# Gate and up by Strassen's seven products on token halves, and T5 biases loaded from DRAM by each mixer

## Chip, cores and metric

One core of a Trainium2 chip. The metric is the device time of one execution in microseconds, the median of the runs. Matmuls run on TensorE (PE in the profile, its weight loads PEld), elementwise work on VectorE (DVE), ScalarE (ACT) and GpSimd (POOL); SyncE (SP) issues most DMAs.

## The reference, cut to what matters

Two blocks run behind each other on 512 tokens of 1024 channels. The first has two layers, each a feed-forward, a mixer of three attentions, and a second feed-forward; the second block (adaptive norms, two more mixers, squared-ReLU networks) is not touched by the change, except for the pools that its first tiles come from.

```python
def _swiglu(x, w_gate, w_up, w_down):
    return (jax.nn.silu(x @ w_gate) * (x @ w_up)) @ w_down      # w_gate, w_up: 1024 x 2816

for l in range(DEPTH):                                          # DEPTH = 2
    x = x + 0.5 * _swiglu(_rmsnorm(x, ffn1_norm[l]), ffn1_w_gate[l], ffn1_w_up[l], ffn1_w_down[l])
    h = _rmsnorm(x, mix_norm[l])
    ...                                                         # three attentions, two with a T5 bias table
    x = x + jnp.concatenate([out_a, out_b, out_c], axis=-1) @ w_out[l]
    x = x + 0.5 * _swiglu(_rmsnorm(x, ffn2_norm[l]), ffn2_w_gate[l], ffn2_w_up[l], ffn2_w_down[l])
```

## The kernel before, in words

The activations lie transposed, eight chunks of 128 channels by 512 tokens. Every float32 product is made of three matmuls of a reduced float32 type (`mm3`, L136): weight and activation are each split in a rounded part (hi) and the rest (lo), and hi x hi, hi x lo and lo x hi are summed in PSUM. `weights` (L144) loads a weight block of 128 x 1024 into a ring of three raw tiles, casts hi on ACT (L149) and subtracts lo on DVE (L142), each in rings of two.

`ffn` (L357) runs 22 steps `up(f)` over the blocks of 128 hidden units. A step loads a gate and an up block, makes 8 chunks x 3 matmuls of 512 columns for each, and `gated` multiplies both by the norm's row factor R, applies Silu to the gate, multiplies, and splits the product into hi and lo (five DVE operations of 512 and two of ACT, counting the split). After 9, 17 and 22 steps `down` multiplies the finished hidden blocks into the eight output chunks; `residual` (L340) adds each to x and, in the last `down`, `push` (L319) makes hi and lo of the next norm's input (L323 on ACT, L325 on DVE) and adds its squares (ACT, then POOL for chunks 1 to 5, DVE for the others). There are four feed-forwards, so 88 steps `up` and 96 output chunks of `down`.

Beside this, `pump` takes a step of background work after each step f > 0 and before each chunk of the first two `down`s: first and foremost `adaln`, 96 units of a DMA of 512 KB and two DVE passes over 1024 elements (L832), which the second block needs; and, from step 2 of the very first feed-forward on, `bias_tables`, which spreads the T5 table over diagonals (DVE copies at L258), writes it skewed to DRAM and reads it back into two persistent tiles `bias_a` and `bias_b` (24 KB a partition), both DMAs on ACT's queue (L267 is the read). `mixer1` uses these tiles. The order in which instructions stand on each engine is made by a planner from program order and readiness, not by hand; each engine then works strictly in that order, and a tile's slot is taken again when its last reader is done.

Of the kernel before, what the change touches and what calls it, by code (L numbers as in the profile page):

```python
# [17 lines left out]
T = 512  # L18
# [106 lines left out]
class Net:  # L125
    def __init__(self, tc, ins, out):
        self.tc, self.nc, self.ins, self.out = tc, tc.nc, ins, out
        self.bg = []
        self.pre = None


    def mm(self, ps, lhsT, rhs, start, stop):
        self.nc.tensor.matmul(ps, lhsT, rhs, start=start, stop=stop)  # L133

    def mm3(self, ps, w, x, start, stop):
        (wh, wl), (xh, xl) = w, x  # L136
        self.mm(ps, wh, xh, start, False)
        self.mm(ps, wh, xl, False, False)
        self.mm(ps, wl, xh, False, stop)
# [4 lines left out]
    def weights(self, src, kc, m=128):  # L144
# [7 lines left out]
        return [(hi[:, k * m:(k + 1) * m], lo[:, k * m:(k + 1) * m]) for k in range(kc)]  # L152

# [85 lines left out]
    def bias_tables(self):  # L239

        nc, tc = self.nc, self.tc
        LA, LB = 384, 640
        with tc.tile_pool(name="boot", bufs=1, reuse_waits="tile") as bp:
# [4 lines left out]
            for L, top, h0, dmax, dst, n in ((LA, 255, 0, 128, self.bias_a, 256), (LB, 511, 8, 512, self.bias_b, 512)):  # L248
                v = bp.tile([128, 8, L], F32, name="v")
# [4 lines left out]
                while d < dmax:  # L254
                    e = d
                    while e < dmax and bk[e] == bk[d]:
                        e += 1
                    nc.vector.tensor_copy(v[:, :, top - e + 1:top - d + 1],  # L258
                                          tab[:, h0:h0 + 8, bk[d]:bk[d] + 1].to_broadcast([128, 8, e - d]))
                    d = e  # L260
                    if d < 16 and d % 4 == 0:
                        yield
                yield
                for h in range(8):
                    s = self.dp.tile([1, 128 * (L + 1)], F32, name="scr%d_%d" % (L, h))
                    nc.scalar.dma_start(s.rearrange("o (p l) -> (o p) l", l=L + 1)[:, :L], v[:, h, :])
                    nc.scalar.dma_start(dst[:, h, :],  # L267
                                        s[:, 127:127 + 128 * L].rearrange("o (p l) -> (o p) l", l=L)[:, :n])
                    if h % 4 == 3:
                        yield  # L270
# [47 lines left out]
    def push(self, d, g):  # L318

        nc = self.nc  # L320
        x = self.x[:, d, :]
        hi = self.xsp.tile([128, T], F32R, name="xs")
        nc.scalar.activation(hi, x, AF.Copy, scale=self.vecs[:, g + d:g + d + 1])  # L323
        lo = self.xsp.tile([128, T], F32R, name="xs")
        nc.vector.scalar_tensor_tensor(lo, x, self.vecs[:, g + d:g + d + 1], hi.bitcast(F32),  # L325
                                       op0=OP.mult, op1=OP.subtract)
        self.xn.append((hi, lo))
# [5 lines left out]
        else:  # L333
            (nc.gpsimd if d < 6 else nc.vector).tensor_tensor(self.acc[:, :T], self.acc[:, :T], sq, op=OP.add)

# [3 lines left out]
    def residual(self, d, ps, scale, g):  # L339
        self.nc.vector.scalar_tensor_tensor(self.x[:, d, :], ps, scale, self.x[:, d, :], op0=OP.mult, op1=OP.add)  # L340
        if g == "final":
            self.square_acc(self.lat, d)
            if d == 0:
                self.acc2 = self.xsp2.tile([128, T], F32, name="xslat", bufs=16)
# [12 lines left out]
    def ffn(self, l, which, nxt, hook=None):  # L357
        nc = self.nc
        gu, dn = self.ins["gu%d" % which], self.ins["dn%d" % which]
        with ExitStack() as es:  # L360
            ap = es.enter_context(self.tc.tile_pool(name="act", bufs=20, reuse_waits="tile"))
# [5 lines left out]
            h, late = {}, []  # L367
            R = y = None

            def up(f):  # L370
                nonlocal R, y
                ws = self.pre or [self.weights(gu[l, f, i], 8) for i in range(2)]
                self.pre = None
                ps = [self.psum(), self.psum()]
                if f == 0:
                    for k in range(8):
                        for w, p in zip(ws, ps):
                            self.mm3(p, w[k], xs[k], k == 0, k == 7)
                    y = self.rstd_y(self.acc, 4, D)
                    late.append((0, ps))  # L380
                    return
                for w, p in zip(ws, ps):
                    for k in range(8):
                        self.mm3(p, w[k], xs[k], k == 0, k == 7)
                if f == 1:
                    R = self.rstd_rows(y, 4)
                    gated(*late.pop())
                gated(f, ps)

            def gated(f, ps):  # L390
# [1706 lines left out]
```

## Time and profile before

| | us |
|---|---|
| median of 3 runs | 3663.9 (3657.01 to 3667.29) |
| the profiled execution | 3660.74 |
| its span from first to last instruction | 3658.7 |
| PE busy | 3576.8 |
| DVE busy | 2235.9 |
| ACT busy | 1492.9 |
| POOL busy | 165.9 |

In time the first block's feed-forwards run from 0 to 380, 612 to 976 and 976 to 1338, and 1571 to 1930 us; its mixers lie between, at 380 to 612 and 1338 to 1571; the rest is the second block. Busy time of PE is modelled, since matmuls overlap: the distance between starts says what one costs in a stream. DVE's and ACT's instructions that follow without a wait begin before the one ahead has ended, so there too starts are compared. A window's line gives the busy time and the number of instructions of each engine in that stretch, and the granted clock of TensorE, 1.00 for 2.4 GHz and 0.50 for 1.2 GHz.

### The profile page before, as it was taken

What the parts mean: (1) busy time and instruction counts of PE and PEld (TensorE: products, weight loads), DVE (VectorE), ACT (ScalarE), POOL (GpSimd) and SP (SyncE); (2) the same over time, 40 slices, a digit from 0 to 9 for tenths busy, and PEclk for the clock granted to TensorE, in tenths of its full rate; (3) what the DMA queues carried; (4) which work ended last, traced back from release to release, by engine and by line L of the source; (5) the groups of instructions that cost most, each with busy time, mean ns of one, the idle gap of its engine ahead of it and who ended that gap; (6) DMA issues with size and microseconds to landing.
All of it is one profiled execution on the core that took longest, in us unless ns stands there. A gap on an engine that the chain in (4) does not pass through costs nothing.

```text
span 3658.7 us, 47782 instructions
## 1 busy us (share of the span) xinstructions
PE 3576.8 (98%) x18706; PEld 3036.4 (83%) x18706; DVE 2235.9 (61%) x4146; ACT 1492.9 (41%) x2562; POOL 165.9 (5%) x186
## 2 busy tenths in 40 slices
PE   8999999999999999999999999999999989999999
PEld 6888887888888888878888888888888878798887
DVE  6576696767676649765446776643333578875443
ACT  4223574322322247542234656532122357763222
POOL 1000002000000010110000000100000101010000
PEclk9999999999999999999999999999999999999999
DMA  6354322445344432133332002111111310022222
GB/s 228 118 165 144 98 70 87 160 147 175 128 157 155 160 116 78 57 115 95 97 96 87 35 30 73 58 61 61 64 64 64 109 44 19 24 70 98 98 98 92
DMA packets 115473, 356.52 MB, mean 97 GB/s; under 512 B 12464, under 2 KB 23088, under 8 KB 114736
## 3 DMA queue, kind: packets, MB, share of 16 engines
q1 hardware_dynamic: 106432, 341.32, 28.2%
q10 hardware_dynamic: 8816, 12.15, 1.1%
q8 instruction: 147, 2.41, 0.3%
q14 instruction: 78, 0.64, 0.1%
HBM read 340.84 MB, written 12.58 MB: 97 GB/s over the span
## 4 chain that ended last, share of the span: by engine, by line
PE 89%; DVE 6%; ACT 3%; issue 1%; DMA 1%; ACTq 0%; SPq 0%; DVEq 0%
PE mm L133 77%; PE o L133 4%; PE s L133 4%; PE pt L1136 1%; DVE wlo L142 1%; PE mm L1749 1%; PE pt L662 1%; PE pt L133 1%; DVE xs L325 0%; ACT whi L149 0%; DVE u L883 0%; DVE xslat L885 0%; PE mm L1032 0%; DVE m L610 0%; ACT s L1743 0%
## 5 line engine op out<-in xcount | busy, mean ns | idle before, releaser
L133 PE MATMUL mm<-xs,whi 128*128 128x512 f32 (+1 forms) x3840 | 1189.7, 391 | 11.8 <-ACT whi L149 8.5
L149 ACT CAST whi<-wraw 128x1024 fp32r<-128x1024 f32 (+3 forms) x528 | 542.1, 1027 | 1583.2 <-PE mm L133 1261.5
L133 PEld LDWEIGHTS mm<-xs,whi 128*128 128x128 f32 x3840 | 717.6, 189 | 160.1 <-ACT whi L149 10.3
L133 PE MATMUL mm<-h,whi 128*128 128x512 f32 (+1 forms) x2944 | 820.8, 371 | 2.0 <-ACT whi L149 2.0
L142 DVE TENSOR_TENSOR wlo<-wraw,whi 128x1024 fp32r<-128x1024 f32 (+3 forms) x528 | 631.5, 1196 | 299.7 <-ACT whi L149 295.2
L133 PE MATMUL mm<-xs,wlo 128*128 128x512 f32 (+1 forms) x1920 | 748.3, 390 | 7.8 <-DVE wlo L142 7.7
L133 PEld LDWEIGHTS mm<-h,whi 128*128 128x128 f32 x2944 | 535.0, 188 | 108.7 <-ACT whi L149 2.2
L133 PE MATMUL mm<-h,wlo 128*128 128x512 f32 (+1 forms) x1472 | 515.4, 371 | 2.1 <-DVE wlo L142 2.1
L133 PEld LDWEIGHTS mm<-xs,wlo 128*128 128x128 f32 x1920 | 362.5, 189 | 87.0 <-DVE wlo L142 12.7
L133 PE MATMUL mm<-xslat,whi 128*128 128x512 f32 x1024 | 333.7, 403 | 6.6 <-DVE xslat L885 2.6
L133 PEld LDWEIGHTS mm<-h,wlo 128*128 128x128 f32 x1472 | 263.8, 188 | 42.6 <-DVE wlo L142 2.7
L832 DVE CUSTOM_DVE_ANT_0 junk<-wraw,silu_c 128x1024 f32<-128x1024 f32 x192 | 234.7, 1222 | 95.2 <-DMA wraw<-in_ada_w 93.8
L911 DVE SCALAR_TENSOR_TENSOR x<-mm,mod,x 128x512 f32<-128x512 f32 (+1 forms) x96 | 67.7, 706 | 282.3 <-PE mm L133 282.3
L133 PE MATMUL mm<-xslat,wlo 128*128 128x512 f32 x512 | 203.4, 398 | 0.7 <-DVE wlo L142 0.7
L133 PEld LDWEIGHTS mm<-xsctx,whi 128*128 128x128 f32 x944 | 171.6, 189 | 37.7 <-ACT w L1100 2.6
L133 PEld LDWEIGHTS mm<-xslat,whi 128*128 128x128 f32 x1024 | 167.2, 189 | 37.4 <-DVE xslat L885 5.4
L133 PE MATMUL mm<-xsctx,whi 128*128 128x256 f32 x944 | 191.6, 286 | 0.7 <-ACT w L1100 0.6
L340 DVE SCALAR_TENSOR_TENSOR x<-mm,x 128x512 f32<-128x512 f32 x144 | 99.2, 689 | 132.0 <-PE mm L133 131.9
L394 DVE TENSOR_TENSOR t<-mm,R 128x512 f32<-128x512 f32 x88 | 60.8, 691 | 138.4 <-PE mm L133 138.3
L392 DVE TENSOR_TENSOR t<-mm,R 128x512 f32<-128x512 f32 x88 | 60.7, 690 | 134.4 <-PE mm L133 134.4
L133 PE MATMUL mm<-xsctx,wlo 128*128 128x256 f32 x472 | 132.9, 282 | 0.0
L133 PEld LDWEIGHTS mm<-xslat,wlo 128*128 128x128 f32 x512 | 97.3, 190 | 7.1 <-DVE wlo L142 1.6
(397 smaller groups left out, 4622.7 us busy)
## 6 DMA issues: line engine op xcount, KB each, us to landing
wraw<-in_gu SPq DMA_DIRECT2D x176, 512.0 KB, 3.6
wraw<-in_mlp_w SPq DMA_DIRECT2D x136, 512.0 KB, 3.4
wraw<-in_ada_w SPq DMA_DIRECT2D x96, 512.0 KB, 3.5
wraw<-in_dn SPq DMA_DIRECT2D x64, 512.0 KB, 3.6
wraw<-in_win SPq DMA_DIRECT2D x30, 512.0 KB, 3.5
wraw<-in_dn SPq DMA_DIRECT2D x32, 384.0 KB, 3.1
wraw<-in_ewin SPq DMA_DIRECT2D x18, 512.0 KB, 3.4
wraw<-in_wo SPq DMA_DIRECT2D x16, 512.0 KB, 3.7
```

Source lines behind the costliest of these rows:

```text
L133: self.nc.tensor.matmul(ps, lhsT, rhs, start=start, stop=stop)
L142: self.nc.vector.tensor_tensor(out, x, hi.bitcast(F32), op=OP.subtract)
L149: nc.scalar.copy(hi, raw)
L340: self.nc.vector.scalar_tensor_tensor(self.x[:, d, :], ps, scale, self.x[:, d, :], op0=OP.mult, op1=OP.add)
L392: nc.vector.tensor_mul(zg, ps[0], R)
L394: nc.vector.tensor_mul(zu, ps[1], R)
L662: nc.tensor.transpose(pt[:, k * 128:(k + 1) * 128], u["s"][:, k * 128:(k + 1) * 128], self.ident)
L832: nc.vector.tensor_tensor_reduce(j, w, self.silu_c[:, c, :], 1.0, 0.0, op0=OP.mult, op1=OP.add, accum_out=self.mod[:, l, f, c:c + 1])
L911: self.nc.vector.scalar_tensor_tensor(s.chunk(d), p, self.mod[:, l, k + d, s.cond:s.cond + 1], s.chunk(d), op0=OP.mult, op1=OP.add)
L1136: nc.tensor.transpose(out, in_, self.ident[:in_.shape[0], :in_.shape[0]])
L1749: nc.tensor.transpose(p[:, b * 256 + e * 128:b * 256 + e * 128 + 128], u[e][:, (2 * g + b) * 128:(2 * g + b + 1) * 128], self.ident)
```

## The change

A step `up(f)` computes gate and up as one product of a 2 x 2 block matrix. Columns of the blocks are the two halves of the 512 tokens on one side and even and odd chunks of channels on the other; rows are gate and up. Strassen's scheme in Winograd's form then takes seven products of half the inner length (four chunks) on 256 tokens each, instead of eight. `sums` loads the gate and the up block, forms four sums of weight quarters on POOL and splits 3.5 blocks instead of two into hi and lo; the raw ring grows to four tiles, the hi and lo rings to three, and a new ring of two holds the sums. `push_sums` forms the matching differences of activations, per pair of chunks, and splits seven half-token tiles. In `up` the products accumulate in three PSUM banks, ACT copies four intermediate results out between them (`keep`), and the seventh product and the gating are put off (`late`) until after the first product of the next step. R is applied to the sum, and by a second multiplication to the Silu's result.

Apart from that, the bias tables are built in four pieces of four heads; only their skewed form in DRAM is kept, and each `mixer1` loads the 16 blocks from the SP queue at its start into a pool of its own. Several tiles of `mixer1` move into pools that the feed-forwards also use, the second block's split inputs get a pool for each stream, and the background work is drained before the last `down` of both feed-forwards of layer 1.

```diff
+    def sums(self, src):
+        nc = self.nc
+        raw = [self.wraw.tile([128, 1024], F32, name="wraw") for _ in range(2)]
+        for t, r in zip(raw, src):
+            nc.sync.dma_start(t, r)
...
+        sa, sb = [self.ssp.tile([128, 1024], F32, name="s") for _ in range(2)]
...
+        for o, a, b, op in ((s1, a21, a22, OP.add), (s2, s1, a11, OP.subtract), (s4, a12, s2, OP.subtract),
+                            (s3, a11, a21, OP.subtract)):
+            nc.gpsimd.tensor_tensor(o, a, b, op=op)
...
+            nc.scalar.copy(hi, x)
+            self.lo(lo, x, hi)
...
+        g, ws = split(raw[0]), {}
+        ws["a11"], ws["a12"] = g[0::2], g[1::2]
+        g = split(sa)
+        ws["s1"], ws["s2"] = g[:4], g[4:]
+        g = split(sb)
+        ws["s4"], ws["s3"] = g[:4], g[4:]
+        ws["a22"] = split(a22, 512)
+        return ws
...
     def push(self, d, g):
...
+        if VCOL["mix_norm"] <= g < VCOL["ffn2_norm"]:
...
+        else:
+            self.push_sums(d, x, gain)
...
+    def push_sums(self, d, x, gain):
+        def split(n, v):
+            t = self.xsp.tile([128, T], F32R, name="xs")
+            nc.scalar.copy(t[:, :H], v)
+            self.lo(t[:, H:], v, t[:, :H])
...
+        def minus(n, a, b):
+            t = self.dif.tile([128, H], F32, name=n)
+            nc.vector.tensor_sub(t, a, b)
+            split(n, t)
...
+        nc.scalar.activation(v, x, AF.Copy, scale=gain)
+        if d % 2 == 0:
+            self.xn.append({})
+            split("b11", v[:, :H])
+            self.even = v, minus("t1", v[:, H:], v[:, :H])
+        else:
+            e, t1 = self.even
+            split("b21", v[:, :H])
+            t2 = minus("t2", v[:, H:], t1)
+            minus("t3", v[:, H:], e[:, H:])
+            split("b22", v[:, H:])
+            minus("t4", v[:, :H], t2)
...
             def up(f):
-                ws = self.pre or [self.weights(gu[l, f, i], 8) for i in range(2)]
-                ps = [self.psum(), self.psum()]
...
-                for w, p in zip(ws, ps):
-                    for k in range(8):
-                        self.mm3(p, w[k], xs[k], k == 0, k == 7)
+                ws = self.pre or self.sums(gu[l, f])
+                pa, pb, pc = [self.psum()[:, :H] for _ in range(3)]
+                def product(p, w, n, more=False):
+                    for j in range(4):
+                        self.mm3(p, ws[w][j], xs[j][n], j == 0 and not more, j == 3, skip_group_check=more)
+                def keep(n, p):
+                    t = sp.tile([128, H], F32, name=n, bufs=2)
+                    nc.scalar.copy(t, p)
+                    return t
+                product(pa, "a11", "b11")
+                t1 = keep("k1", pa)
+                while late:
+                    late.pop()()
+                product(pc, "s1", "t1")
+                t5 = keep("k5", pc)
+                product(pb, "a12", "b21")
+                product(pa, "s2", "t2", True)
+                t2 = keep("k2", pa)
+                product(pc, "s4", "b22", True)
+                product(pa, "s3", "t3", True)
+                t3 = keep("k3", pa)
+                def last():
+                    product(pa, "a22", "t4", True)
...
+            def gated(f, pa, pb, pc, t1, t2, t3, t5):
                 zg, zu = self.tmp(), self.tmp()
-                nc.vector.tensor_mul(zg, ps[0], R)
+                nc.vector.tensor_add(zg[:, :H], pb, t1)
+                nc.vector.tensor_add(zg[:, H:], pc, t2)
+                nc.vector.tensor_mul(zg, zg, R)
                 nc.scalar.activation(zg, zg, AF.Silu)
-                nc.vector.tensor_mul(zu, ps[1], R)
-                nc.vector.tensor_mul(zu, zu, zg)
+                nc.vector.tensor_mul(zg, zg, R)
+                nc.vector.tensor_mul(zu[:, :H], pa, zg[:, :H])
+                nc.gpsimd.tensor_tensor(t3, t3, t5, op=OP.add)
+                nc.vector.tensor_mul(zu[:, H:], t3, zg[:, H:])
...
+    def load_biases(self, pool):
+        self.bias_a = pool.tile([128, 8, 256], F32, name="bias_a")
+        self.bias_b = pool.tile([128, 8, 512], F32, name="bias_b")
+        for i, (s, L) in enumerate(self.skewed):
+            dst, n = (self.bias_a, 256) if i < 8 else (self.bias_b, 512)
+            self.nc.sync.dma_start(dst[:, i % 8, :],
+                                   s[:, 127:127 + 128 * L].rearrange("o (p l) -> (o p) l", l=L)[:, :n])
...
     def mixer1(self, l, nxt):
+            self.load_biases(es.enter_context(tc.tile_pool(name="bias", bufs=1, side="right", reuse_waits="tile")))
...
-            self.wraw, self.whi, self.wlo = pool("wraw", 3), pool("whi", 2), pool("wlo", 2)
+            self.wraw, self.whi, self.wlo = pool("wraw", 4), pool("whi", 3), pool("wlo", 3)
```

## Rows read from the trace of the kernel before

**Rows 1.** The page: busy time by engine, and the chain that ended last.

```profile
PE 3576.8 (98%) x18706; PEld 3036.4 (83%) x18706; DVE 2235.9 (61%) x4146; ACT 1492.9 (41%) x2562; POOL 165.9 (5%) x186
...
PE 89%; DVE 6%; ACT 3%; issue 1%; DMA 1%; ACTq 0%; SPq 0%; DVEq 0%
```

**Rows 2.** Windows: two steps `up` (with, without background work), then half-token matmuls.

```profile
core 0: us, PE busy (x) PEld busy (x) DVE busy (x) ACT busy (x) POOL busy (x), PEclk, DMA share, GB/s
199.40:210.28 10.88, 10.88 (x49) 9.01 (x49) 7.33 (x10) 3.26 (x5) 0.00 (x0) 1.00 0.43 143
1727.60:1738.48 10.88, 10.88 (x49) 9.01 (x48) 5.04 (x7) 3.26 (x5) 0.00 (x0) 1.00 0.32 95
3253.28:3256.16 2.88, 2.88 (x27) 2.88 (x26) 1.71 (x2) 1.36 (x2) 0.00 (x0) 1.00 0.02 6
```

**Rows 3.** Timeline of DVE in one step: start us, us, operation, idle before.

```profile
201.32 1.22 DVE L142 TENSOR_TENSOR wlo<-wraw,whi 128x1024 fp32r<-128x1024 f32 x1
202.46 1.22 DVE L832 CUSTOM_DVE_ANT_0 junk<-wraw,silu_c 128x1024 f32<-128x1024 f32 x1
...
205.66 0.69 DVE L395 TENSOR_TENSOR t<-t 128x512 f32<-128x512 f32 x1
206.27 1.22 DVE L142 TENSOR_TENSOR wlo<-wraw,whi 128x1024 fp32r<-128x1024 f32 x1
```

**Rows 4.** Groups by line and shape: count, busy us, mean ns, idle before.

```profile
L149 ACT CAST whi<-wraw 128x1024 fp32r<-128x1024 f32 x478 | 502.3, 1052 | 1489.3 <-PE mm L133 1211.6 <-issue 242.4 <-DMA scr<-v 12.3
L1587 ACT COPY kraw<-mm 128x256 f32<-128x256 f32 x24 | 9.2, 381 | 2.6 <-DVE v L1586 2.4
...
L142 DVE TENSOR_TENSOR wlo<-wraw,whi 128x1024 fp32r<-128x1024 f32 x478 | 586.3, 1227 | 284.2 <-ACT whi L149 279.9
L1601 DVE TENSOR_TENSOR kraw<-kraw,gy 128x256 f32<-128x256 f32 x24 | 8.4, 419 | 0.1
```

**Rows 5.** Timelines of DVE and POOL at the mixer's end and at 1602 us.

```profile
599.04 0.74 DVE L325 SCALAR_TENSOR_TENSOR xs<-x,vecs,xs 128x512 fp32r<-128x512 f32 x1
...
600.64 1.81 DVE L325 SCALAR_TENSOR_TENSOR xs<-x,vecs,xs 128x512 fp32r<-128x512 f32 x1
602.38 0.68 DVE L340 SCALAR_TENSOR_TENSOR x<-mm,x 128x512 f32<-128x512 f32 x1
602.98 1.21 DVE L142 TENSOR_TENSOR wlo<-wraw,whi 128x1024 fp32r<-128x1024 f32 x1
...
600.62 1.30 POOL L334 TENSOR_TENSOR acclat<-acclat,t 128x512 f32<-128x512 f32 x1 [21.47 <-ACT t L329]
...
1603.14 1.76 DVE L142 TENSOR_TENSOR wlo<-wraw,whi 128x1024 fp32r<-128x1024 f32 x1
...
1602.95 0.86 POOL L868 TENSOR_TENSOR accctx<-accctx,t 128x256 f32<-128x256 f32 x1 [33.81 <-ACT t L867]
```

**Rows 6.** Windows: the end of a mixer, behind it, and the end of a feed-forward.

```profile
600.04:611.37 11.33, 8.76 (x35) 5.96 (x33) 11.33 (x13) 8.34 (x13) 7.53 (x5) 1.00 0.34 118
611.40:613.60 2.20, 0.38 (x3) 0.33 (x3) 2.20 (x4) 1.68 (x4) 0.00 (x0) 1.00 0.31 127
613.70:617.00 3.30, 3.30 (x10) 2.55 (x9) 2.00 (x4) 2.89 (x2) 0.00 (x0) 0.50 0.52 159
...
597.40:611.40 14.00, 11.43 (x47) 8.14 (x45) 13.68 (x17) 10.26 (x16) 7.53 (x5) 1.00 0.37 130
...
352.00:380.00 28.00, 28.00 (x125) 23.20 (x124) 16.84 (x23) 14.39 (x22) 9.93 (x11) 1.00 0.57 179
```

**Rows 7.** Background work and biases: groups, one line's instructions, DMA issues, waits.

```profile
L832 DVE CUSTOM_DVE_ANT_0 junk<-wraw,silu_c 128x1024 f32<-128x1024 f32 x192 | 234.7, 1222 | 95.2 <-DMA wraw<-in_ada_w 93.8
...
L258 DVE COPY v<-tab x64: 160/177/1818, 15.1 to 54.0; 128x8 f32<-128x8 f32 x32, 128x24 f32<-128x24 f32 x6, 128x32 f32<-128x32 f32 x4, 128x48 f32<-128x48 f32 x4
...
L651 DVE CUSTOM_DVE_ANT_0 s<-s,bias_a,sink x64: 344/480/485, 447.5 to 1457.6; 128x256 f32<-128x256 f32 x48, 128x128 f32<-128x128 f32 x16
...
bias_b<-scr ACTq DMA_DIRECT2D x8, 256.0 KB, 4.2
...
ACT whi L149 <- DMA bias_a<-scr: 6.3, 1, 6.3
```

More of the change, by code (lines that the diff above doesn't have):

```diff
@@ L129, in __init__, with mm, mm3 @@
         self.pre = None
[L132 to L135 removed]
+        self.chunks = {}
+    def mm(self, ps, lhsT, rhs, start, stop, **k):
+        self.nc.tensor.matmul(ps, lhsT, rhs, start=start, stop=stop, **k)
+    def mm3(self, ps, w, x, start, stop, **k):
         (wh, wl), (xh, xl) = w, x
[L137 to L139 removed]
+        self.mm(ps, wh, xh, start, False, **k)
+        self.mm(ps, wh, xl, False, False, **k)
+        self.mm(ps, wl, xh, False, stop, **k)
     def lo(self, out, x, hi):
@@ L152, in weights, with split @@
         return [(hi[:, k * m:(k + 1) * m], lo[:, k * m:(k + 1) * m]) for k in range(kc)]
+    def sums(self, src):
[3 more added lines that the diff above has]
+            nc.sync.dma_start(t, r)
+        (a11, a12), (a21, a22) = [[t.rearrange("p (j e m) -> p j e m", e=2, m=128)[:, :, e, :] for e in range(2)]
+                                  for t in raw]
+        sa, sb = [self.ssp.tile([128, 1024], F32, name="s") for _ in range(2)]
+        (s1, s2), (s4, s3) = [[t[:, 512 * e:512 * e + 512].rearrange("p (j m) -> p j m", m=128) for e in range(2)]
+                              for t in (sa, sb)]
+        for o, a, b, op in ((s1, a21, a22, OP.add), (s2, s1, a11, OP.subtract), (s4, a12, s2, OP.subtract),
+                            (s3, a11, a21, OP.subtract)):
+            nc.gpsimd.tensor_tensor(o, a, b, op=op)
+        def split(x, n=1024):
+            hi = self.whi.tile([128, 1024], F32R, name="whi")[:, :n]
+            lo = self.wlo.tile([128, 1024], F32R, name="wlo")[:, :n]
+            if n < 1024:
+                hi, lo = [t.rearrange("p (j m) -> p j m", m=128) for t in (hi, lo)]
+            nc.scalar.copy(hi, x)
+            self.lo(lo, x, hi)
+            if n < 1024:
+                return [(hi[:, j, :], lo[:, j, :]) for j in range(4)]
+            return [(hi[:, k * 128:(k + 1) * 128], lo[:, k * 128:(k + 1) * 128]) for k in range(8)]
+        g, ws = split(raw[0]), {}
[6 more added lines that the diff above has]
+        return ws
     def psum(self, name="mm", n=512):
@@ L343, in residual @@
             if d == 0:
-                self.acc2 = self.xsp2.tile([128, T], F32, name="xslat", bufs=16)
+                self.acc2 = self.chunks["ctx"].tile([128, T], F32, name="acc2")
                 self.nc.scalar.activation(self.acc2, self.x[:, d, :], AF.Square, scale=self.vec("final_norm", d))
@@ L366, in ffn @@
                 hook(es)
-            h, late = {}, []
+            h, late, first = {}, [], []
+            sp = es.enter_context(self.tc.tile_pool(name="sums", bufs=1, reuse_waits="tile"))
             R = y = None
+            H = T // 2
             def up(f):
                 nonlocal R, y
-                ws = self.pre or [self.weights(gu[l, f, i], 8) for i in range(2)]
+                ws = self.pre or self.sums(gu[l, f])
                 self.pre = None
-                ps = [self.psum(), self.psum()]
+                pa, pb, pc = [self.psum()[:, :H] for _ in range(3)]
[5 more added lines that the diff above has]
+                    nc.scalar.copy(t, p)
+                    return t
+                product(pa, "a11", "b11")
[12 more added lines that the diff above has]
+                    product(pa, "a22", "t4", True)
+                    if f == 0:
+                        first.append((0, pa, pb, pc, t1, t2, t3, t5))
+                    else:
+                        gated(f, pa, pb, pc, t1, t2, t3, t5)
+                late.append(last)
@@ L425, in ffn @@
                 up(f)
-            if hook is not None:
+            late.pop()()
+            if l:
                 self.drain()
@@ L878, in modulate @@
             if new:
-                s.xs.append([self.xsp.tile([128, s.m], F32R, name="xs" + s.name, bufs=16) for _ in range(2)])
+                s.xs.append([self.chunks[s.name].tile([128, s.m], F32R, name="xs" + s.name, bufs=16) for _ in range(2)])
             hi, lo = s.xs[d]
@@ L1365, in split @@
             def split():
-                return [[self.xsp.tile([128, s.m], F32R, name="xs" + s.name, bufs=16) for _ in range(2)] for s in (lat, ctx)]
+                return [[self.chunks[s.name].tile([128, s.m], F32R, name="xs" + s.name, bufs=16) for _ in range(2)] for s in (lat, ctx)]
             ob = [split() for _ in range(4)]
@@ L1906, in block1 @@
             nc.sync.dma_start(self.x[:, 0, :], ins["xT"][0])
-            self.pre = [self.weights(ins["gu1"][0, 0, i], 8) for i in range(2)]
+            self.ssp = pool("s", 2, reuse_waits="tile")
+            self.pre = self.sums(ins["gu1"][0, 0])
             for d in range(8):
```

93 lines of the change are left out of this document (45 added, 48 removed).

## The prediction

> **What bounds the kernel now.** I read the page's busy shares and chain first. PE is busy 98% of the span and carries 89% of the chain [rows 1], so nearly everything else is hidden behind matmuls. Then the windows over one step `up(f)` (one gate block and one up block, 48 matmuls of 512 columns): the step lasts 10.88 us, 227 ns a matmul, PE never idles, and neither the step with background work (DVE busy 7.33 us) nor the one without (5.04 us) is shorter [rows 2]. There are 88 such steps, some 957 us, a quarter of the span. So the question is what a step costs afterwards on each engine, and which of them is then the slowest.
>
> **PE.** Seven products of 4 chunks and 3 matmuls are 84 matmuls of 256 columns in place of 48 of 512. Columns fall by an eighth, but the price per matmul is not half: in the half-token matmuls at 3253 us, 24 take 2.88 us, 120 ns each, and the weight-load row is busy the whole 2.88 us, where beside 512 columns it has 1.87 us of 10.88 free [rows 2]. 84 x 0.120 = 10.08 us, a gain of 0.80 us a step, 70 us over 88.
>
> The Trainium skill, "TensorE: Matmul & The Clock Gate", Back-to-back issue gap, gives 262 cycles at 2.4 GHz for 256 columns; an estimate from it is 109 ns, 9.2 us a step and a gain of 148 us. The row is taken instead, since it has the weight loads in it.
>
> **ACT.** Before, two casts of 1024 (1.05 us), the Silu and the hi copy give 3.26 us a step [rows 2, 4]. After: three casts of 1024, one of 512 and four evacuations of 256 at 0.38 us [rows 4]: 3.26 + 1.05 + 0.6 + 1.5 = 6.4 us of 10. Not a bound.
>
> **DVE.** Added are one subtraction of 1024 and one of 512, and the gating goes from three operations of 512 on the products to two of 512 and four of 256. Back to back, a 1024 subtraction takes 1.14 us (201.32 to 202.46) and a 512 one 0.61 us (205.66 to 206.27) [rows 3]; a 256 one takes 0.42 us by itself, some 0.38 in a queue [rows 4]. So 1.14 + 0.61 + 4 x 0.38 - 0.69 = 2.6 us more: 9.9 us a step with background work, 7.6 us without. The background work is 96 units of two passes of 1.22 us over a table block, 192 passes [rows 7]; by the order of the code's calls 42 fall into `down` and 54 into `up`. So in 54 steps DVE alone is about as long as PE, and in 34 it is not.
>
> **POOL, and what it does to DVE.** The four sums of a block (512 elements each) and the addition `t3 + t5` (256) go to POOL, idle in these steps now [rows 2]. The rows show that POOL and a DVE operation with two SBUF inputs exclude each other: the subtraction in `push` takes 0.74 us at 599.04, but 1.81 us at 600.64, where it begins with a POOL addition of 512 that lasts 1.30 us, and ends 0.53 us behind it; a weight subtraction of 1024 takes 1.76 us instead of 1.23 beside a POOL addition of 256 [rows 3, 5]. So a POOL operation of 512 costs a waiting DVE 1.07 us, one of 256 0.53 us, and a step 4 x 1.07 + 0.53 = 4.8 us if it always hits. DVE operations with one input in PSUM keep their time in these rows; after the change only three short ones of a step are of that sort (1.2 of 9.9 us), everything else reads SBUF twice. How much of the 4.8 us is paid is read from the stretch that is nearest, 600.04 to 611.37, where DVE never stops [rows 6]: its own operations are six residuals at 0.60 (602.38 to 602.98) [rows 5], six `push` subtractions at 0.74 less the 0.08 by which queued ones overlap, and one weight subtraction at 1.14, 8.7 us; it lasts 11.33, so five POOL operations (5.35 us at full price) cost some 2.6 us, 48%, with 41% of DVE's own time in residuals that read PSUM. With 12% instead of 41%, 0.48 / 0.59 x 0.88 = 72%, 3.5 us a step. Bounds: 48% (2.3 us) and all (4.8 us).
>
> The Trainium skill, "SBUF — State Buffer", SBUF: two separate sides, calls this an exclusive lock held for the whole instruction. By that rule one would charge POOL's whole durations, some 6.1 us a step, as an estimate 2 us more on each DVE-bound step; the rows show that a waiting operation's start-up overlaps, so 4.8 us is the end taken here.
>
> **What a step becomes.** With background work 9.9 + 3.5 = 13.4 us; without, 7.6 + 3.5 = 11.1 us. To this come waits for buffers: three slots for weight tiles serve four tiles a step, so the tile of the next `a11`/`a12` can be cast only when product `s2` is done, two products (2.9 us) before it is needed, and cast plus subtraction alone are 2.3 us [rows 4]; DVE's queue stands in that gap. I add 0.3 to 0.4 us and take 13.7 and 11.5. Sum: 54 x (13.7 - 10.9) + 34 x (11.5 - 10.9) = 151 + 20 = 171 us. Bounds: 12.2 and 10.3 (48% paid, no buffer waits) give 51 us; 14.8 and 12.5 (all paid) give 265 us.
>
> **The other parts.** (a) `push_sums` replaces `push` before four of the six norms that block 1 pushes: per pair of chunks 11 DVE operations of 256 instead of 2 of 512, 11 x 0.36 - 2 x 0.67 = 2.6 us, 10.4 us a series. At the mixers' ends DVE is already the bound, busy 13.68 of 14.00 us [rows 6]: 12 us each with more POOL hits, 24. At the end of the second feed-forward DVE is busy 16.8 of 28 us [rows 6], so only the last chunk's chain shows: 4 us. At the start most of the series lies on the path behind the input loads: 9 us. (b) The bias tables are built from four pieces of four heads: 64 copies become 128, at 0.18 us 11 us more [rows 7], and their old cover, an idle DVE in the first 54 us, is gone: 12 us. (c) Each mixer loads 16 blocks, 3 MB, from the SP queue ahead of its saves and projection weights. Their first use is 67 us after the mixer begins at 380 us [rows 7]; what can wait is the weight queue behind them. 3 MB are 22 us at a step's 143 GB/s [rows 2], and up to three weight blocks loaded ahead feed PE for 16 us: 0 to 22 us, of which I take 4 each, near the covered end since one block lands in 4 us [rows 7]: 8. (d) The bias loads leave ACT's queue, where a cast waited 6.3 us for one [rows 7]; steps there still took 10.88 us, so nothing is gained. The changed pools, the missing table load in the last feed-forward and the earlier drain: nothing, they sit beside full PE stretches. Sum of (a) to (d): 57 us, between 20 and 90.
>
> **The sum.** 171 + 57 = 228 us on the profiled execution's 3660.7 us: 3889. The median of the runs shown is 3.2 us above that execution, so I write 3890 for the median. Bounds: 3660.7 + 51 + 20 = 3732, and 3660.7 + 265 + 90 = 4016.
>
> **Rivals.**
> *PE sets the pace* (chance 0.08, faster): the POOL sums slip between DVE's operations and background work yields. Then 70 us are gained and some 20 lost at the ends: 3611. For it: POOL's sums depend on nothing but loads. Against it: DVE alone needs 9.9 us and the blocked rows.
> *DVE's own time sets the pace, POOL is free* (0.08, the same): 54 steps near 10.5 and 34 near 10.1 us, -48 us, and +57 from the rest: 3670. Decides if the collision hits only `push`-like pairs; against it stands the weight subtraction of 1.76 us.
> *PE's waits also cost clock* (0.12, slower still): a step would idle PE some 3.6 us, and behind a stretch in which PE worked 0.38 of 2.20 us the granted clock was 0.50, 1.2 GHz, for the next 3.3 us [rows 6]. One such fall a step loses half of 3.3 us of PE work; where it lies on the path, 54 x 1.7 = 92 us: 3980, 4040 with all 88 steps.
> *The sums aren't made ahead* (0.02): if POOL's chain of four sums, 1.3 to 2 us each, starts only when a step's products end, each step shows some 8 us more: 4500. The change would then not do what it says; two sum buffers and four raw ones speak against it.
>
> **How the numbers follow.** The forecast, DVE and POOL serialised in the steps, has 0.70. 3890 is its time. The range takes its bounds, 3732 at the low end, and reaches up over the clock rival to 4060; left out are the two cases that are not slower and the last, 0.18. A measurement here tells some 0.3%, 11 us, from no change. Faster 0.08, same 0.08, slower 0.84.
>
> **What would show it.** In windows over `up` steps: PE no longer full, 84 matmuls of 120 ns where they run back to back, DVE busy over 95% in steps with background work, steps near 13.7 and 11.5 us; weight subtractions of 1024 stretched from 1.23 toward 2.2 us where a POOL sum overlaps; PE's waits put down to `wlo`. `down` unchanged at 24 x 0.227 = 5.4 us a block. The prediction fails if the subtractions keep 1.23 us beside POOL sums, or if steps with background work come out at 10 to 11 us; it fails the other way if PE's waits go to `whi` casts or raw loads.

## The result, and the profile after

The changed kernel takes 3860.6 us (median of 4 runs, 3859.4 to 3865.2), the kernel before 3665.0 us in the same comparison: ratio 1.054, 95% interval 1.0522 to 1.0559. It is slower, at the predicted place (3890, range 3732 to 4060). The profiled execution took 3861.35 us, its span is 3859.6 us.

First the page, the busy line and the chain, which answer to [rows 1]:

```profile
PE 3597.7 (93%) x21874; PEld 3179.9 (82%) x21874; DVE 2768.4 (72%) x4794; ACT 1773.0 (46%) x3201; POOL 842.3 (22%) x629
...
PE 70%; DVE 19%; issue 4%; ACT 4%; DMA 2%; POOL 1%; ACTq 0%; DVEq 0%; SPq 0%; POOLq 0%
```

PE carried 89% of the chain and carries 70% now; DVE went from 6% to 19%. Second the windows over steps `up`, from one gating to the next, as in [rows 2] (us, busy time and instructions of each engine, granted clock, DMA share, GB/s): two steps with background work, one without.

```profile
core 0: us, PE busy (x) PEld busy (x) DVE busy (x) ACT busy (x) POOL busy (x), PEclk, DMA share, GB/s
247.12:260.90 13.78, 10.72 (x78) 10.51 (x77) 13.38 (x16) 5.97 (x10) 7.07 (x6) 0.88 0.34 114
904.49:918.33 13.84, 12.63 (x103) 12.11 (x102) 13.70 (x16) 7.09 (x12) 7.22 (x6) 1.00 0.33 114
...
1959.41:1970.74 11.33, 10.26 (x85) 9.94 (x84) 11.19 (x12) 5.84 (x11) 7.02 (x6) 1.00 0.27 94
```

13.8 and 11.3 us in place of 10.88, DVE busy 97 to 99% of each, PE no longer full, POOL 7 us. Third the timeline of DVE in the middle one, with POOL's operations of that time, the answer to [rows 3] and [rows 5] (start us, us, operation, idle before):

```profile
904.82 1.99 DVE L950 CUSTOM_DVE_ANT_0 junk<-wraw,silu_c 128x1024 f32<-128x1024 f32 x1
...
906.74 1.22 DVE L143 TENSOR_TENSOR wlo<-wraw,whi 128x1024 fp32r<-128x1024 f32 x1
...
908.93 1.76 DVE L143 TENSOR_TENSOR wlo<-s,whi 128x1024 fp32r<-128x1024 f32 x1
...
911.40 1.33 DVE L499 TENSOR_TENSOR t<-k,t 128x256 f32<-128x256 f32 x1
912.65 0.41 DVE L497 TENSOR_TENSOR t<-mm,t 128x256 f32<-128x256 f32 x1
912.98 1.98 DVE L950 CUSTOM_DVE_ANT_0 junk<-wraw,silu_c 128x1024 f32<-128x1024 f32 x1
...
916.63 1.78 DVE L143 TENSOR_TENSOR wlo<-wraw,whi 128x512 fp32r<-128x512 f32 x1
```

```profile
903.98 1.75 POOL L169 TENSOR_TENSOR s<-wraw 128x512 f32<-128x512 f32 x1
908.68 0.93 POOL L498 TENSOR_TENSOR k<-k,k 128x256 f32<-128x256 f32 x1 [2.96 <-ACT k L461]
910.83 1.61 POOL L169 TENSOR_TENSOR s<-wraw 128x512 f32<-128x512 f32 x1 [1.22 <-DVE wlo L143]
912.52 1.36 POOL L169 TENSOR_TENSOR s<-s,wraw 128x512 f32<-128x512 f32 x1
916.25 1.60 POOL L169 TENSOR_TENSOR s<-wraw,s 128x512 f32<-128x512 f32 x1 [2.37 <-DVE wlo L143]
```

Each POOL operation has a DVE operation that lasts longer than usual and ends 0.3 to 1.1 us behind it, as if its own work began only then: 1.99 and 1.98 instead of 1.22, 1.76 instead of 1.22, 1.33 instead of 0.42, 1.78 instead of 0.69. Together 4.1 us; the step less these is 9.7 us. In the step without background work the same sum is 3.8 us of 11.3.

Over the whole span the groups say the same (count, busy us, mean ns, idle before), against 1227 and 1222 ns in [rows 4, 7]:

```profile
L143 DVE TENSOR_TENSOR wlo<-wraw,whi 128x1024 fp32r<-128x1024 f32 x390 | 505.0, 1295 | 272.5 <-ACT whi L150 256.3 <-ACT whi L176 10.5
...
L950 DVE CUSTOM_DVE_ANT_0 junk<-wraw,silu_c 128x1024 f32<-128x1024 f32 x192 | 283.6, 1477 | 41.2 <-DMA wraw<-in_ada_w 40.5
...
L143 DVE TENSOR_TENSOR wlo<-s,whi 128x1024 fp32r<-128x1024 f32 x176 | 246.5, 1402 | 18.6 <-ACT whi L176 18.1
...
L143 DVE TENSOR_TENSOR wlo<-wraw,whi 128x512 fp32r<-128x512 f32 x88 | 118.6, 1348 | 5.9 <-ACT whi L176 5.5
```

and PE's waits (first block; us in total, times, longest) are put down to `wlo`, DVE's result, while the casts hardly wait for POOL's sums:

```profile
PEld mm L134 <- DVE wlo L143: 145.6, 98, 3.5
PE mm L134 <- DVE wlo L143: 124.7, 91, 3.3
...
ACT whi L176 <- POOL s L169: 25.1, 14, 2.2
```

So it is not that the sums come late: of 176 casts of a sum, 14 waited for one.

Where the 201 us of span lie, from the starts of the `residual` operations, which both kernels have in the same order (after less before, us; "steps" runs from the end of the `down` or mixer ahead to the first residual, "chunks" from the first to the eighth):

| | steps 0-8 | chunks | steps 9-16 | chunks | steps 17-21 | chunks |
|---|---|---|---|---|---|---|
| layer 0, first ffn | 36.8 | 2.4 | 15.2 | 3.0 | 8.4 | 0.9 |
| layer 0, second | 25.6 | 4.5 | 18.4 | 2.8 | 8.0 | 7.4 |
| layer 1, first | 21.9 | 4.5 | 16.7 | 3.6 | 1.8 | 0.9 |
| layer 1, second | 18.6 | 2.4 | 0.7 | 2.5 | 0.3 | 0.9 |

Sum 208; the mixers add 2.6 each, the second block gives 12.6 back.

### The profile page after: what moved, and what is told of

It reads as the page before. It is cut to its first block, busy times and chain, and to the rows that moved or that the text cites. A ratio compares the mean times of both kernels' runs of the same rounds, so it can differ in the third digit from the quotient of the medians.

```text
span 3859.6 us, 56432 instructions
## 1 busy us (share of the span) xinstructions
PE 3597.7 (93%) x21874; PEld 3179.9 (82%) x21874; DVE 2768.4 (72%) x4794; ACT 1773.0 (46%) x3201; POOL 842.3 (22%) x629
## 4 chain that ended last, share of the span: by engine, by line
PE 70%; DVE 19%; issue 4%; ACT 4%; DMA 2%; POOL 1%; ACTq 0%; DVEq 0%; SPq 0%; POOLq 0%
PE mm L134 59%; DVE wlo L143 7%; PE o L134 4%; PE s L134 3%; DVE junk L950 2%; DVE xs L143 1%; PE pt L1254 1%; DMA wraw<-in_ada_w 1%; PE mm L1867 1%; PE pt L779 1%; DVE t L390 1%; DVE t L499 1%; DVE h L143 1%; DVE t L496 1%; POOL s L169 1%
## 5 line engine op out<-in xcount | busy, mean ns | idle before, releaser
L134 PE MATMUL mm<-xs,whi 128*128 128x256 f32 (+1 forms) x5956 | 1266.4, 310 | 72.7 <-ACT k L461 26.4
L134 PEld LDWEIGHTS mm<-xs,whi 128*128 128x128 f32 x5956 | 987.4, 197 | 128.0 <-ACT k L461 33.1
L134 PE MATMUL mm<-xs,wlo 128*128 128x256 f32 (+1 forms) x2978 | 925.2, 311 | 125.4 <-DVE wlo L143 125.0
L143 DVE TENSOR_TENSOR wlo<-wraw,whi 128x1024 fp32r<-128x1024 f32 (+4 forms) x528 | 667.6, 1266 | 298.1 <-ACT whi L150 275.8
L150 ACT CAST whi<-wraw 128x1024 fp32r<-128x1024 f32 (+3 forms) x352 | 356.7, 1014 | 895.5 <-PE mm L134 712.3
L134 PEld LDWEIGHTS mm<-xs,wlo 128*128 128x128 f32 x2978 | 585.6, 197 | 164.8 <-DVE wlo L143 145.3
L169 POOL TENSOR_TENSOR s<-wraw 128x512 f32<-128x512 f32 x176 | 291.8, 1661 | 455.7 <-DMA wraw<-in_gu 272.0
L176 ACT CAST whi<-s 128x1024 fp32r<-128x1024 f32 x176 | 184.1, 1047 | 270.2 <-PE mm L134 184.5
L143 DVE TENSOR_TENSOR wlo<-s,whi 128x1024 fp32r<-128x1024 f32 x176 | 246.5, 1402 | 18.6 <-ACT whi L176 18.1
L176 ACT CAST whi<-wraw 128x1024 fp32r<-128x1024 f32 (+1 forms) x176 | 146.9, 836 | 136.7 <-PE mm L134 118.8
```

The lines of the kernel that those rows point to most:

```text
L134: self.nc.tensor.matmul(ps, lhsT, rhs, start=start, stop=stop, **k)
L143: self.nc.vector.tensor_tensor(out, x, hi.bitcast(F32), op=OP.subtract)
L150: nc.scalar.copy(hi, raw)
L169: nc.gpsimd.tensor_tensor(o, a, b, op=op)
L176: nc.scalar.copy(hi, x)
```

## Experiments

Theory A is the prediction's: DVE sets the step and POOL's operations add to its time by excluding it. Theory B: slots and the strict order of the engines set it. Theory C: PE's waits cost TensorE clock.

**POOL's operations left out.**

```diff
-        for o, a, b, op in ((s1, a21, a22, OP.add), (s2, s1, a11, OP.subtract), (s4, a12, s2, OP.subtract),
-                            (s3, a11, a21, OP.subtract)):
-            nc.gpsimd.tensor_tensor(o, a, b, op=op)
+        sa = sb = raw[1]
...
-                nc.gpsimd.tensor_tensor(t3, t3, t5, op=OP.add)
```

> The changed kernel without POOL's part of a step: the four weight sums and t3 + t5 are left out (the products that should read a sum read the up block instead; the number of casts, subtractions and matmuls stays). Theory A (DVE sets the step, and POOL's operations add to DVE's time by excluding it): steps fall to DVE's own 9.9 us or PE's 10.1 us, 10.1 to 10.5 us with and without background work. From the measured averages of the stretches, 13.2 and 11.2 us: 54 x 2.9 + 34 x 1.0 = 190 us less, about 3670 us. Theory B (the step is set by slots: three hi and lo tiles for four splits, two sum tiles, with engines that work strictly in order): the splits and their slots are the same, so steps stay above 12 us and the time above 3780 us. Theory C (the waits cost TensorE clock): the clock rises from 0.979 and some 90 us come back at most.

Measured 3664.5 us, ratio to before 1.0006 (0.9997 to 1.0015): the whole loss is gone. Windows over a step with and one without background work:

```profile
223.50:234.50 11.00, 10.44 (x87) 10.15 (x86) 9.71 (x17) 6.05 (x11) 0.00 (x0) 1.00 0.41 144
1776.60:1786.90 10.30, 10.30 (x87) 10.11 (x86) 7.81 (x12) 5.94 (x11) 0.00 (x0) 1.00 0.31 102
```

DVE's own time is 9.71 and 7.81 us (forecast 9.9 and 7.6). Without background work PE is full again, 10.3 us. The 11.0 with it has 1.2 us in which DVE waits for a table block's load:

```profile
231.00 1.23 DVE L944 CUSTOM_DVE_ANT_0 junk<-wraw,silu_c 128x1024 f32<-128x1024 f32 x1 [1.22 <-DMA wraw<-in_ada_w]
```

B falls for the hi and lo slots: casts, subtractions and the rings of three are unchanged. The two sum tiles are gone as well; that they don't set the step is shown by the next experiment, which keeps them. And PE's gain is small even where nothing hinders it: some 0.6 us a step, which `push_sums` and the bias tables eat.

**POOL's operations moved to DVE.**

```diff
-            nc.gpsimd.tensor_tensor(o, a, b, op=op)
+            nc.vector.tensor_tensor(o, a, b, op=op)
...
-                nc.gpsimd.tensor_tensor(t3, t3, t5, op=OP.add)
+                nc.vector.tensor_tensor(t3, t3, t5, op=OP.add)
```

> The changed kernel with the four weight sums and t3 + t5 on DVE instead of POOL. Theory A: DVE's own time becomes 9.9 + 4 x 0.61 + 0.38 = 12.7 us a step with background work and 10.4 us without, and nothing excludes it any more; against 13.7 and 11.4 us that is 1 us a step less, 88 us in all, about 3770 us (3750 to 3800). Rival (POOL's time is mostly hidden, DVE only happens to be busy): 2.8 us more a step, 4000 us or more. Theory B: no change or slower, since the same slots wait in a longer DVE queue.

Measured 3773.4 us, ratio 1.0302 (1.0285 to 1.0319), 87 us less than with POOL.

```profile
226.00:238.30 12.30, 10.77 (x87) 10.25 (x87) 12.22 (x21) 6.17 (x11) 0.00 (x0) 1.00 0.42 128
1887.20:1897.50 10.30, 10.30 (x86) 10.09 (x86) 10.05 (x17) 5.90 (x12) 0.00 (x0) 1.00 0.31 102
```

Five additions done by DVE itself cost it 2.5 us (12.22 less 9.71); done by POOL they cost DVE 4.1. The rival, that POOL's time is mostly hidden, falls.

**Each sum issued twice.**

```diff
-            nc.gpsimd.tensor_tensor(o, a, b, op=op)
+            for _ in range(2):
+                nc.gpsimd.tensor_tensor(o, a, b, op=op)
```

> The changed kernel with each of the four POOL sums issued twice in a row. Theory A: a further sum costs DVE what the first cost, between 0.5 and 1.07 us, 0.77 us by the forecast's share: 4 x 0.77 x 88 = 270 us more, about 4130 us (4035 to 4235). If POOL and DVE did not exclude each other, POOL's eight sums of 1.3 us and one of 0.7 us, 11.1 us, would fit beside steps of 11.3 to 13.8 us and the time would hardly move (3860 to 3890).

Measured 4189.8 us, ratio 1.144 (1.142 to 1.146), 329 us more than with single sums.

```profile
301.10:318.80 17.70, 13.11 (x84) 12.82 (x84) 17.56 (x16) 6.09 (x11) 15.88 (x10) 0.81 0.29 90
2244.90:2260.50 15.60, 11.07 (x87) 10.24 (x86) 14.94 (x13) 5.89 (x10) 15.29 (x10) 1.00 0.20 68
```

A step grows by 3.9 (with background work) and 4.2 us (without): 0.96 to 1.05 us for each further sum, so the full price of 1.07 us rather than the 72% expected. POOL itself is nearly full here (15.29 of 15.60 us without background work), blocked by DVE in turn; so this is the price when two engines take turns and either could be called the bound, not one that holds for the single sums.

The Trainium skill, "SBUF — State Buffer", SBUF: two separate sides, calls this an exclusive lock for the whole instruction. The exclusion agrees with the rows; the price doesn't quite: a sum lasts 1.28 us where nothing blocks it (below, from the changed kernel) and costs DVE 1.0.

```profile
1778.78 1.28 POOL L169 TENSOR_TENSOR s<-wraw 128x512 f32<-128x512 f32 x1 [1.22 <-issue]
```

**Background work left out.**

```diff
-                for c in range(2):
-                    j = self.junk.tile([128, D], F32, name="junk")
-                    nc.vector.tensor_tensor_reduce(j, w, self.silu_c[:, c, :], 1.0, 0.0, op0=OP.mult, op1=OP.add,
-                                                   accum_out=self.mod[:, l, f, c:c + 1])
```

> The changed kernel without the 192 DVE passes over the table blocks (their DMAs stay). Theory A: all steps come out like those without background work, 11.2 to 11.5 us: 54 x (13.2 - 11.2) = 108 us less, and a little more at the starts of the feed-forwards, about 3745 us (3725 to 3765). If the slots or the clock set the step, DVE's load doesn't matter and the time stays near 3850 us.

Measured 3763.8 us, ratio 1.0278 (1.0259 to 1.0296), 97 us less. Steps 9 to 16 of the three feed-forwards that had background work fall from 13.8 to 11.3 to 11.6 us, 15 to 18 us per eight. DVE's load sets the step.

**`push_sums` replaced by `push`.**

```diff
-        v = self.dif.tile([128, T], F32, name="v%d" % (d % 2))
-        nc.scalar.activation(v, x, AF.Copy, scale=gain)
...
+        self.nc.scalar.activation(hi, x, AF.Copy, scale=gain)
+        lo = self.xsp.tile([128, T], F32R, name="xs")
+        self.nc.vector.scalar_tensor_tensor(lo, x, gain, hi.bitcast(F32), op0=OP.mult, op1=OP.subtract)
+        a, b = (hi[:, :H], lo[:, :H]), (hi[:, H:], lo[:, H:])
...
```

> The changed kernel with push_sums replaced by the old two operations a chunk (the products take halves of these tiles in place of the differences, so the number of matmuls stays). The forecast priced push_sums at 37 us (two mixers' ends 24, a feed-forward's end 4, the start 9): 3824 us. The stage comparison of the two traces leaves some 57 us for the four beginnings beyond what their steps explain, of which the bias tables have a part in the first: between 3803 and 3824 us. If push_sums is hidden at these places, 3860 us.

Measured 3827.6 us, ratio 1.0452 (1.0432 to 1.0471), 33 us less than the changed kernel and just above the expected range. From the residuals: the start 4 us, the two mixers' ends with the steps behind them 8 and 13, the end of layer 0's second feed-forward with the next start 11.

**One product less.**

```diff
-                product(pa, "s3", "t3", True)
```

> The changed kernel with one product of the seven (s3) left out: 72 matmuls a step, 8.64 us of PE instead of 10.08; DVE's, ACT's and POOL's work is unchanged. Theory A (PE doesn't set the step, save in the first step of each of the 12 stretches, whose weights are ready): 12 x 1.44 = 17 us less at most, 3843 to 3862 us. If PE still set part of each step: up to 88 x 1.44 = 127 us less, 3735 us.

Measured 3879.5 us, ratio 1.0592 (1.0571 to 1.0613): 19 us slower with a seventh of the PE work of a step gone, outside both cases. That the amount of PE's work doesn't set the step is shown; why it got slower is only partly clear.

```profile
1974.30:1986.30 12.00, 9.34 (x72) 8.73 (x72) 10.64 (x12) 5.92 (x12) 6.93 (x5) 1.00 0.26 87
1986.30:1998.70 12.40, 10.77 (x72) 10.16 (x72) 9.61 (x12) 5.94 (x12) 6.93 (x5) 0.86 0.25 86
```

DVE is not full here. Its timeline in the first of these windows, and a line of the waits over four steps (1962 to 2010 us):

```profile
1980.39 2.28 DVE L143 TENSOR_TENSOR wlo<-s,whi 128x1024 fp32r<-128x1024 f32 x1 [1.32 <-ACT whi L176]
```

```profile
ACT k L461 <- PE mm L134: 11.8, 4, 3.8
```

DVE waits 1.3 us a step for a cast, and ACT works in order, with a `keep` in its queue that waits 3 us a step for its product. So here waits in the engines' strict order, theory B, do lengthen the step. The steps at full clock last 12.0 us too, so a fallen clock (0.957 on the mean, 0.979 in the changed kernel) is not all of it. How much each has, and what the planner's other order does, stays open.

**POOL additions put into the kernel before.**

```diff
+            for _ in range(2):
+                nc.gpsimd.tensor_tensor(pool.tile([128, 512], F32, name="s"), raw[:, :512], raw[:, 512:], op=OP.add)
```

> The kernel before with four POOL additions of 512 elements a step added, over the raw weight tiles and with a result that nobody reads. Theory A (POOL's operations lengthen DVE's, but only DVE's slack pays as long as it has some): DVE's 7.33 us in a step with background work become 9.3 to 11.6 of 10.88 us, its 5.04 us at most 9.3; steps stay at 10.9 us, 3665 to 3685 us. Rival (a collision delays the subtraction on which the next matmuls wait, whatever the load): 1 us or more a step, 3750 us or more.

Measured 3711.2 us, ratio 1.0132 (1.0117 to 1.0147): above the forecast. The edit stands in `weights` and runs for both blocks of a step. Windows over eight steps, without and with background work, and over a feed-forward's beginning:

```profile
1763.00:1850.00 87.00, 87.00 (x385) 72.09 (x384) 51.47 (x49) 25.61 (x31) 32.99 (x24) 1.00 0.31 97
775.00:862.00 87.00, 85.44 (x371) 68.77 (x370) 67.07 (x85) 25.04 (x31) 43.40 (x28) 1.00 0.43 145
621.00:731.00 110.00, 103.78 (x445) 82.77 (x445) 93.90 (x109) 36.45 (x44) 58.70 (x38) 0.98 0.42 139
```

Without background work nothing is lost (the stretch differs by 0.0 us), with it 2 to 4 us per eight steps, and 32 of the 45 us of span lie in the four beginnings (11, 6, 6 and 9 us), where the norm's `push` adds to DVE's work (93.9 of 110 us in the last window, 73.8 of 105.3 in the kernel before). So POOL's operations cost nothing where DVE has much slack (51.5 of 87 us busy), and a little already at 67 of 87; the miss is that I looked at the steps and forgot the beginnings. Even there DVE is not full, and it waits for table blocks, whose DMAs need a slot of the ring of three raw tiles that POOL's additions read too (this kernel in the last window, then the kernel before from 608.3 to 713.6 us):

```profile
DVE junk L836 <- DMA wraw<-in_ada_w: 11.2, 7, 2.0
```

```profile
DVE junk L832 <- DMA wraw<-in_ada_w: 5.3, 2, 2.7
```

How much of the 32 us is DVE's lengthened work and how much the ring, this run doesn't tell apart.

**The T5 part alone.** The edit is the change's `bias_tables`, `load_biases` and the sinks' pool, in the kernel before.

> The kernel before with the T5 part of the change alone: tables built in four pieces, their skewed form kept in DRAM, 16 blocks loaded by each mixer from the SP queue. The forecast priced it at 20 us in the changed kernel, 12 for the tables and 8 for the loads; here the tables have their cover, an idle DVE, so by the same reasoning only the loads remain, 8 us: 3673 us. Rival: the loads are hidden as well, and the waits of ACT for bias loads in the first 60 us go away: 3655 to 3666 us.

Measured 3698.3 us, ratio 1.0096 (1.0081 to 1.011): some 37 us, far more than either case. The mixers, where the loads are, differ by 0.9 and 0.2 us up to their first residual, so the loads cost next to nothing. The time is spread evenly over stretches in which PE never waits: 2.2 us per eight steps, 1.0 us per `down` of eight blocks. Every matmul of 512 columns had become slower. The edit also moved the sinks (128 bytes a partition) from the far side of SBUF to a place between the weight tiles and all tiles behind them. The next experiments are about that.

**Only the place in SBUF.** The kernel before with 128 unused bytes at that place (32 columns, shown; 64 columns for 256 bytes), and the changed kernel with the sinks below the weights.

```diff
+            pool("pad", 1).tile([128, 32], F32, name="pad")
             self.rp = pool("R", 2, reuse_waits="tile")
```

```diff
+            self.bt = pool("sinks", 1)
             self.xp = pool("x", 1)
```

> The kernel before with an unused tile of 128 bytes a partition between the weight tiles (whi, wlo) and the tiles behind them (R, xs, tmp, act); nothing else. In the T5-only kernel these tiles moved up by the same 128 bytes (the sinks' pool, 4 x (16 + 8 + 8) bytes, was put ahead of them), every matmul of 512 columns in the feed-forwards took 232.4 ns instead of 226.7, and the time rose by 37 us. Theory P (the distance in SBUF between a matmul's weights and its moving tile sets 227 or 232 ns): 232.4 ns here too, some 35 us more, 3690 to 3702 us. Theory Q (the T5 loads or their traffic did it): no change, 3655 to 3668 us.

> The same with 256 bytes. Under theory P the distance becomes 256 bytes more. If any shift counts, or 512 bytes is the period, 232 ns and 3690 to 3702 us; if the period is 256 bytes, 227 ns and 3655 to 3668 us. Under theory Q no change.

> The changed kernel with the sinks' 128 bytes put below the weight tiles instead of between them and xs and act, so that weights and moving tiles stand as they did before the change (distance 0 instead of 128 modulo 512). Theory P: matmuls of 512 columns in down at 227 instead of 232.4 ns, 12 x 1 us of down and a little in the first step of each stretch, 12 to 20 us less, 3840 to 3850 us; the steps in which DVE is the bound keep their length. Theory Q: no change, 3860 us.

Measured: 128 bytes 3698.4 us, ratio 1.010 (1.0084 to 1.0115); 256 bytes 3662.1 us, 1.0003 (0.9994 to 1.0012); the changed kernel 3851.3 us instead of 3860.6, 1.052 (1.0506 to 1.0534), 9 us less where 12 to 20 were expected. That interval overlaps the changed kernel's (1.0522 to 1.0559); the starts of matmuls below do not depend on it. Matmuls that start in 80 us of full PE (165 to 245 us), in the kernel before with 128 and with 256 bytes:

```profile
165.00:245.00 80.00, 80.00 (x345) 64.35 (x344) 51.20 (x71) 23.18 (x29) 0.00 (x0) 1.00 0.42 143
```

```profile
165.00:245.00 80.00, 80.00 (x355) 66.26 (x354) 54.80 (x76) 24.59 (x30) 0.00 (x0) 1.00 0.44 146
```

345 against 355 at the same granted clock of 1.00; the mean distance of starts in `down` (from the first residual to the eighth, over 7 x 24 matmuls) is 233.3 against 226.7 ns, and 232.4 in the T5-only kernel. The same in a `down` of the changed kernel, first as it is, then with the sinks below the weights:

```profile
320.00:345.00 25.00, 25.00 (x109) 20.26 (x109) 17.64 (x23) 5.33 (x6) 5.96 (x4) 1.00 0.64 212
```

```profile
324.00:349.00 25.00, 25.00 (x112) 20.71 (x111) 17.04 (x23) 5.26 (x5) 6.05 (x4) 1.00 0.64 210
```

For the first block theory P holds: 0 and 256 bytes are fast, 128 slow. In the last run the moving tiles stand where they stood in the slow kernel and the weights have moved, so it is the place of one to the other and not that of the moving tile alone. Of the changed kernel's 196 us some 9 are this.

**The same for the second block of the kernel before.** There `xslat` stands 96 bytes off, and its matmuls of 512 columns take 233 ns.

```diff
+        self.xs_stack.enter_context(self.tc.tile_pool(name="pad", bufs=1, side="right")).tile([128, 24], F32, name="pad")
         self.xsp2 = self.xs_stack.enter_context(self.tc.tile_pool(name="xs2", bufs=1, side="right", reuse_waits="tile"))
```

> The kernel before with 96 unused bytes ahead of the second block's input tiles, so that xslat and xsctx stand at the same distance to the weight tiles as the feed-forwards' xs (0 instead of 96 modulo 512). Theory P: the 1536 matmuls of 512 columns with xslat fall from 233 to 227 ns, 9 us less on a path that PE sets, and perhaps a little in those of 256 columns: ratio 0.997 to 0.998, about 3652 us. Theory Q: no change.

Measured 3660.1 us, ratio 0.9997 (0.9988 to 1.0006): no change that can be told. These matmuls take 232.4 ns now (median 231), 233.0 before (median 232), not 227; so theory P as put fails there, and what the condition is stays open. No version tried beats the kernel before.

## Why the prediction was right, and where it wasn't

**PE.** 84 matmuls of 120 ns were right: with PE full the step lasts 10.3 us. The estimate from the Trainium skill, "TensorE: Matmul & The Clock Gate", Back-to-back issue gap, 9.2 us from a figure for the isolated matmul, is not what the traces show; the row with the weight loads in it was the better guide.

**DVE and POOL.** The mechanism is shown by four experiments: without POOL's operations the loss is gone, on DVE they cost 87 us less, doubled they cost 329 us more, and without background work 97 us go. The sizes: DVE's own 9.7 and 7.8 us (9.9 and 7.6), POOL's charge 4.1 and 3.8 us by the lines, 4.0 and 3.4 by DVE's busy time with and without POOL's operations (3.5 for both), buffer waits about none (0.3 to 0.4). So three terms were off by 0.2 to 0.6 us and cancelled: 13.8 and 11.4 us a step, forecast 13.7 and 11.5. Blocked subtractions of 1024 reach the 2.2 us named as a sign, and more; over the whole span 26 of 566 last 2.2 us or longer, the others that are blocked mostly 1.7 to 2.0:

```profile
1172.69 2.32 DVE L143 TENSOR_TENSOR wlo<-s,whi 128x1024 fp32r<-128x1024 f32 x1
```

The 72% in POOL's charge came out near the measured 70 to 85% by luck. I counted six residuals and six `push` subtractions between 600.04 and 611.37 us; there are five of each: a residual at 600.04, one of either in [rows 5], and the others here (the last line is the window's end):

```profile
604.12 1.78 DVE L325 SCALAR_TENSOR_TENSOR xs<-x,vecs,xs 128x512 fp32r<-128x512 f32 x1
605.82 0.68 DVE L340 SCALAR_TENSOR_TENSOR x<-mm,x 128x512 f32<-128x512 f32 x1
606.42 1.15 DVE L325 SCALAR_TENSOR_TENSOR xs<-x,vecs,xs 128x512 fp32r<-128x512 f32 x1
607.49 0.68 DVE L340 SCALAR_TENSOR_TENSOR x<-mm,x 128x512 f32<-128x512 f32 x1
608.09 1.66 DVE L325 SCALAR_TENSOR_TENSOR xs<-x,vecs,xs 128x512 fp32r<-128x512 f32 x1
609.68 0.68 DVE L340 SCALAR_TENSOR_TENSOR x<-mm,x 128x512 f32<-128x512 f32 x1
610.28 1.16 DVE L325 SCALAR_TENSOR_TENSOR xs<-x,vecs,xs 128x512 fp32r<-128x512 f32 x1
611.37 0.68 DVE L340 SCALAR_TENSOR_TENSOR x<-mm,x 128x512 f32<-128x512 f32 x1
```

DVE's own work there is 5 x 0.60 + 5 x 0.66 + 1.14 = 7.4 us, not 8.7, and POOL cost it 3.9 us, 73% of the full price and not 48%. Scaling 73% by the share of operations that read SBUF twice, as I did with 48%, gives more than the full price, the upper end of my steps, and some 3980 us in all. So the price, the direction and the mechanism were right, the scaling was wrong, and the miscount hid it.

**The sum over the steps.** A stretch is cheaper than its steady step times its number: eight steps with background work cost 15 to 18 us more than before up to the first residual, where 8 x 2.8 is 22. Part comes back in the first chunks of `down` (2.4 to 4.5 us each time), where I had said "unchanged": the put-off seventh product of a stretch's last step runs behind the first chunk, 12 matmuls of 0.12 or 1.4 us, and 0.9 is the SBUF distance (with the sinks below the weights, 2.4 becomes 1.5).

**The other parts.** (a) `push_sums`: 33 us measured, 37 forecast, but with parts that cancel: the mixers' ends 8 and 13 (12 each), the start 4 (9), the feed-forward's end 11 (4; the 28 us read for it in [rows 6] end layer 0's first feed-forward, not its second). (b) Bias tables: not measured alone; without POOL's work the first beginning is still 11 us longer than before and the others between 8 shorter and 3 longer, so some 10 us fit, 12 forecast. (c) Bias loads: 8 forecast, nothing found; the mixers up to their first residual are 1.3 us shorter. (d) "The changed pools: nothing" failed twice: 128 bytes of displacement cost 9 us, and the second block takes 1717 us instead of 1730. The kernels above that have the changed pools show 1717 to 1721 there, the T5-only kernel, which hasn't, 1731; what does it wasn't tried. The gain comes in four jumps of 2.6 to 4.1 us between the second block's stages, and `xslat`'s matmuls keep their 233 ns, so it isn't the SBUF distance; the larger weight rings, which the second block uses too, are in question beside the pools. Of the 27 us between 228 forecast and 201 measured, the second block thus has 13, the bias loads and mixers 10, `push_sums` 4; the SBUF distance takes 9 the other way, and the rest, an estimate of 8 us from these numbers, lies in the steps.

**The rivals.** PE setting the pace and a free POOL fell with the first three experiments. The clock did fall more often, 0.979 granted against 0.992, but it took no time in these steps: one at 0.88 lasts 13.78 us, one at 1.00 13.84. PE has slack there, and a fall is paid out of it. The sums were made ahead; the time given for the case that they weren't, 4500 us, should have been some 4590 (88 x 8 us on 3890).

**Other slips.** The gating before has four DVE operations of 512, three on the products and the split, not five as its description says; the forecast's sum uses the right number. From POOL's whole durations, 6.1 us, to the 3.5 us taken are 2.6 us a step, not 2. Neither changes the forecast.

## What to carry to other kernels

Before cutting PE work, sum up per step what the other engines must do instead: here DVE's 9.7 us still fitted beside PE's 10.3 (a step of 11.0, most of the rest a wait for a load), its 12.2 didn't. Work that is handed to POOL to relieve DVE is charged to DVE when both read SBUF twice: additions that DVE did in 2.5 us cost it 4.1 us when POOL did them, so on a busy DVE they were better left on DVE. And after any change of pools, compare the distance from start to start of an untouched matmul stream with the one before.

## What the runs showed of the hardware that was not expected

A matmul stream of 512 columns runs at 226.7 or at some 232 ns a matmul, at the same granted clock, with PE never waiting, depending on where weights and moving tiles lie in SBUF to each other. 128 bytes more made it slow in three kernels (T5 only, the padded one, the changed one), 256 bytes more didn't, and moving the weights by the same 128 bytes made it fast again. It is 2.5% of every such stretch, 37 us of 3662. In the second block the same cure did nothing that can be told (233.0 to 232.4 ns).

The background pass, a multiply with a running sum, is blocked by POOL like a plain subtraction: 1.98 us instead of 1.22.
